# Laying out both segments' triangular blocks over partitions ahead of the substitutions

## Chip, cores and metric

One core of one Trainium2 chip. The metric is the device time of one execution in microseconds (us), as the median of several runs. Engines are named as the profile names them: PE (TensorE), DVE (VectorE), ACT (ScalarE), POOL (GpSimd), SP (SyncE, which only issues transfers here).

## What is computed

A backbone of two layers over two segments of tokens: 512 latent tokens ("lat") and 256 context tokens ("ctx"), width 1024. Each layer normalises its input, multiplies it by one combined input projection, feeds three groups of heads from it (a gated DeltaNet, windowed attention with a sink, an HGRN2 recurrence), projects their joined outputs back, adds them to the stream, and runs a squared-ReLU MLP. The context passes through the same weights and leaves its states for the latents; in the second layer only its states are wanted.

The part that matters here is the triangular system of the DeltaNet scan. For each chunk of 64 tokens, each of 4 heads and each of 2 directions:

```python
a = jnp.where(strict, jnp.einsum('bhid,bhjd->bhij', kb, ki) * decay, 0.0) + eye
uw = lax.linalg.triangular_solve(a, rhs, left_side=True, lower=True, unit_diagonal=True)
```

That is a unit triangular matrix of 64 x 64, to be inverted or solved with. ctx has 4 chunks (32 such matrices), lat has 8 (64 of them).

## The kernel before

**Inverting the blocks.** `delta_prep` builds the strict parts of all matrices on PE, ACT and DVE and leaves them, 64 x 64 each, in one buffer `U` (`seg.U`). `delta_inverse` then inverts them for one segment. It cuts each matrix into four blocks of 32 x 32. The two triangular blocks on the diagonal are laid out one matrix block per partition: 8 n of them, with n = 2 x chunks, so 64 partitions for ctx and 128 for lat. This goes through DRAM, on POOL's queue: one transfer of U to `seg.ud` (L1027) and eight small ones back (L1029), four into buffer P and four into Q. POOL also fills buffer Y with identities (L1024, L1025). DVE copies the half in Q over to P, transposed (L1032), and runs a substitution of 31 steps with two instructions each (L1036, L1037) that turns Y into the inverses; a fourth small buffer, tb, holds the products. DVE makes a transposed copy (L1043), and the results go back through DRAM: two transfers out (L1045), eight back into U (L1048) and four that put the partner blocks of the other orientation into a buffer B (L1050). PE and ACT then finish the off-diagonal blocks in two rounds, one per buffer half: products with B (L1067), a copy to a ring H (L1068), products with H (L1071), and the result into U (L1072). Their PSUM banks are 2 and 3 ("ni").

**What runs beside it.** The line that the change touches, in layer 0, gives the planner three streams: the inverses of ctx and then lat; the rest of the input projections for both segments (`project_hg`, `project_gates`: PE products L554 to L556 with weights that ACT and DVE split at L540 and L541, results written to DRAM by POOL at L748 and L791 from two staging buffers); and attention of ctx (`attention(0, ctx)`: eight rounds, each with scores L1384, a softmax, a transposition L1435, the sums L1444 and a final product on DVE, L1446). After these come two streams for ctx: `delta_chain`, four steps that start with L1103 and L1109 and need the inverted blocks, then `delta_norm`; and `hgrn` with `head_norm`, whose first PE work is L1241, with PSUM banks 2 and 3 again ("hg"), and whose end is L828 to L830. After those come lat's `delta_chain` (eight steps, the same lines), the modulation of the next layer (`ada`, PE at L590, its PSUM bank is 2) and the output projection and MLP of ctx in the background.

**What sets the order.** The streams are Python generators. `run` draws from the stream whose virtual time is least, each `yield` advancing it by an estimate of microseconds divided by a speed. This is the order of tracing, and so the default priority; `ahead(g, 3000)` makes a stream's instructions more urgent. A planner then lays all instructions out against a model of their times and fixes one order for each engine and queue. On the chip each engine takes its instructions in that order and waits where an input or a buffer isn't ready. POOL's transfers and fills are one such queue.

**Buffers.** All work buffers come from one arena in blocks of 1 KB a partition (`get`, `free`). `free` notes a running number. `get` takes the stretch whose newest number is lowest, counted from 30 below the current number, and prefers short free stretches. The bookkeeping follows the order of tracing. An instruction that writes into a reused block waits for those that used it before. P, Q, Y take 4 blocks each and tb one; B takes 2 for ctx and 4 for lat; H takes 2 x 2. ctx attention holds 16 blocks in four rings: two for queries, four for probabilities, three pairs for their transposes, four for the row scales (two of these are used in each round).

Of the kernel before, what the change touches and what calls it, by code (L numbers as in the profile page):

```python
# [167 lines left out]
def bc(ap, axis, n):  # L168
    ap = ap.unsqueeze(axis)
    return ap.broadcast_to(list(ap.shape[:axis]) + [n] + list(ap.shape[axis + 1:]))  # L170
# [103 lines left out]
def run(*streams):  # L274

    at = [[0.0, i, g, speed] for i, (g, speed) in enumerate((x if isinstance(x, tuple) else (x, 1.0)) for x in streams)]
    while at:
        a = min(at)
        try:
            a[0] += next(a[2]) / a[3]  # L280
        except StopIteration:
            at.remove(a)
# [22 lines left out]
class Net:  # L305
# [380 lines left out]
    def project(self, l, segs):  # L686

        for seg in segs:
            if seg.x is None:
                self.x_load(seg)  # L690
        pbs = [self.rstd(seg, "n") for seg in segs]
        if l == 0:
            ring = Ring(self, 8, 1024)
            run(self.ada(0, 0, ring))
            ring.free()
        for seg, pb in zip(segs, pbs):
            seg.h = self.modulated(l, 0, seg, pb)
            self.x_free(seg)
            seg.r, seg.b, seg.need = {}, {}, seg is self.lat or l < DEPTH - 1
            if seg is self.ctx:  # L700
                seg.kv0 = l * 256
# [303 lines left out]
        for x in ("dq", "dk", "dv")[i0:]:  # L1005
            seg.b[x].free()

    def delta_inverse(self, seg):


        nc, Uv = self.nc, seg.U
        n, u = 2 * seg.nc, slice(seg.u0, seg.u0 + 2 * seg.nc)
        half, size = slice(4 * n, 8 * n), slice(0, 8 * n)
        Pb, Qb, Yb, tb = self.get(1024), self.get(1024), self.get(1024), self.get(256)
        P, Q, Y = (b.v.rearrange("p (a b) -> p a b", a=32) for b in (Pb, Qb, Yb))

        def quarters():

            for i in range(8):
                fw, hf, jb = i < 4, i // 2 % 2, i % 2  # L1020
                rows = slice(64 * hf + 32 * jb, 64 * hf + 32 * jb + 32)
                yield slice(i * n, i * n + n), hf if fw else 1 - hf, rows, slice(32 * jb, 32 * jb + 32), fw, fw == (jb == 0)

        nc.gpsimd.memset(Yb.v[size], 0.0)  # L1024
        nc.gpsimd.memset(Yb.v[size, 0:1024:33], 1.0)  # L1025

        nc.gpsimd.dma_start(out=seg.ud[:], in_=Uv[:, :, u])  # L1027
        for blk, vv, rows, cols, fw, first in quarters():
            nc.gpsimd.dma_start(out=(P if fw else Q)[blk], in_=seg.ud[rows, vv, :, cols].rearrange("r u i -> u r i"))  # L1029
        yield 8.0  # L1030

        nc.vector.tensor_copy(P[half], Q[half].rearrange("p a b -> p b a"))  # L1032
        for c in range(31):
            m = 31 - c
            t = tb.v[size, :(c + 1) * m].rearrange("p (r m) -> p r m", m=m)
            nc.vector.tensor_tensor(out=t, in0=bc(Y[size, :c + 1, c], 2, m), in1=bc(P[size, c, c + 1:], 1, c + 1), op=ALU.mult)  # L1036
            nc.vector.tensor_tensor(out=Y[size, :c + 1, c + 1:], in0=Y[size, :c + 1, c + 1:], in1=t, op=ALU.subtract)  # L1037
            yield 0.3 + (c + 1) * m / 480
        Pb.free()
        tb.free()  # L1040
        Z, Bb = Q, self.get(2 * n * 32)
        B = Bb.v.rearrange("p (v u i) -> p v u i", v=2, u=n)
        nc.vector.tensor_copy(Z[size], Y[size].rearrange("p a b -> p b a"))  # L1043
        for i, b in enumerate((Yb, Qb)):
            nc.gpsimd.dma_start(out=seg.xd[i], in_=b.v[size].rearrange("p (a b) -> p a b", a=32))  # L1045

        for blk, vv, rows, cols, fw, first in quarters():
            nc.gpsimd.dma_start(out=Uv[rows, vv, u, cols], in_=seg.xd[0 if fw else 1, blk].rearrange("u r i -> r u i"))  # L1048
            if first:
                nc.gpsimd.dma_start(out=B[rows, vv], in_=seg.xd[1 if fw else 0, blk].rearrange("u r i -> r u i"))  # L1050
        yield 10.0
        Qb.free()
        Yb.free()
        Hr = Ring(self, 2, 512)
        for vv in range(2):
            firsts = []
            for hf in range(2):
                a, b = 64 * hf, 64 * hf + 32
                sa, sb = slice(0, 32), slice(32, 64)
                if hf != vv:  # L1060
                    a, b, sa, sb = b, a, sb, sa
                firsts.append((slice(a, a + 32), slice(b, b + 32), sa, sb))
            ph, pu, H = self.bank("ni"), self.bank("ni"), Hr()
            U = Uv[:, vv, u]
            for ra, rb, sa, sb in firsts:
                for k in range(n):
                    nc.tensor.matmul(ph[rb, k * 32:k * 32 + 32], lhsT=U[ra, k, sb], rhs=B[ra, vv, k], start=True, stop=True)  # L1067
                nc.scalar.copy(H[rb, :n * 32], ph[rb, :n * 32])  # L1068
            for ra, rb, sa, sb in firsts:
                for k in range(n):  # L1070
                    nc.tensor.matmul(pu[ra, k * 32:k * 32 + 32], lhsT=H[rb, k * 32:k * 32 + 32], rhs=U[rb, k, sb], start=True, stop=True)  # L1071
                nc.scalar.activation(out=U[ra, :, sb], in_=pu[ra, :n * 32].rearrange("p (u i) -> p u i", i=32), func=AF.Copy, scale=-1.0)  # L1072
            yield 2.0
        Bb.free()
        Hr.free()
# [436 lines left out]
    def run(self, stop=None):  # L1512
        self.setup()
        lat, ctx = self.lat, self.ctx
        both = (ctx, lat)
# [10 lines left out]
        def seq(*gs):  # L1526
            for g in gs:
                yield from g
# [11 lines left out]
        self.reserve((lat, ctx), "sq0", "sq1")  # L1540
        run(self.ahead(prep(0, both), 3000), (self.project_swa(0, both), 0.6), (ada(0, 2), 0.7))
        self.banks = dict(self.BANKS, m=(4, 5, 6), t=None)
        run(self.ahead(seq(self.delta_inverse(ctx), self.delta_inverse(lat)), 3000), (self.ahead(seq(self.project_hg(0, both), self.project_gates(0, both)), -1000), 0.9), (self.attention(0, ctx), 0.5))
        self.banks = self.BANKS
        for seg in both:
            seg.h.free()
# [115 lines left out]
```

## Time and profile before

| | us |
|---|---|
| median of 3 runs | 2117.33 (2115.97 to 2119.23) |
| the profiled execution | 2116.83 |
| its span in the trace | 2115.0 |
| PE busy | 1977.7 |
| DVE busy | 1219.3 |
| ACT busy | 857.6 |
| POOL busy | 144.2 |

Times in the rows are counted from the start of the span. The profiled execution takes 1.8 us more than its span. A busy PE is not a PE at its peak: its matmuls are pipelined, their ends are modelled, and its clock has two levels, 1.2 and 2.4 GHz. The clock that was granted is given as a share of full speed: 1.00 is 2.4 GHz, 0.50 is 1.2 GHz, values between are a stretch with some of both.

### The profile page before, as it was taken

The numbers are of one execution on the slowest core, as the hardware profiler recorded it, in microseconds if no ns is written. First come the engines' busy times: TensorE is split into PE (matmuls) and PEld (weight loads), VectorE is DVE, ScalarE is ACT, GpSimd is POOL, SyncE is SP. The second block draws the span as 40 slices with busy tenths as digits, with TensorE's granted clock in tenths as the row PEclk, the third lists the DMA queues.
The fourth block names the chain that finished last, engine by engine and source line by source line (L and its number), as shares of the span: only waits on it lengthen the run. The fifth ranks groups of instructions, "written<-read, shape, count | busy, mean of one in ns | idle before, by whom it ended". The sixth has DMA issues, their size and how long they took to land.

```text
span 2115.0 us, 37910 instructions
## 1 busy us (share of the span) xinstructions
PE 1977.7 (94%) x15456; PEld 1620.8 (77%) x15456; DVE 1219.3 (58%) x2737; ACT 857.6 (41%) x1703; POOL 144.2 (7%) x281
## 2 busy tenths in 40 slices
PE   5999998799999999699999998999899979999996
PEld 2787887688899898588888876767678747888885
DVE  4574856666976667577333334666887483333334
ACT  2432353235465564353434242324555234334241
POOL 0001231200000000010000000011200000000000
PEclk9999999799999999899999999999999999999998
DMA  8435342145233243243222235464300222222221
GB/s 336 156 111 165 93 130 77 57 163 188 95 111 106 100 147 111 85 151 105 95 100 94 96 113 187 140 186 154 122 20 2 81 70 91 99 98 92 100 90 70
DMA packets 72445, 242.43 MB, mean 115 GB/s; under 512 B 10192, under 2 KB 12368, under 8 KB 72144
## 3 DMA queue, kind: packets, MB, share of 16 engines
q1 hardware_dynamic: 57456, 197.35, 27.7%
q0 software_dynamic: 11792, 34.14, 5.1%
q10 hardware_dynamic: 3024, 8.53, 1.2%
q8 instruction: 121, 1.98, 0.4%
q14 instruction: 52, 0.43, 0.1%
HBM read 218.21 MB, written 19.14 MB: 112 GB/s over the span
## 4 chain that ended last, share of the span: by engine, by line
PE 78%; DVE 9%; DMA 6%; issue 4%; ACT 2%; POOL 1%; ACTq 0%; DVEq 0%; POOLq 0%
PE psum L554 20%; PE psum L556 19%; PE psum L555 19%; PE psum L590 2%; PE psum L1444 2%; DMA arena<-in_ada 1%; PE psum L1435 1%; PE psum L1382 1%; DVE weights L541 1%; PE psum L1109 1%; PE psum L1067 1%; PE psum L1261 1%; DMA arena<-in_ff 1%; PE psum L1071 1%; DVE arena L1272 1%
## 5 line engine op out<-in xcount | busy, mean ns | idle before, releaser
L554 PE MATMUL psum<-r,weights 128*128 128x512 f32 (+1 forms) x2304 | 830.4, 361 | 11.7 <-ACT arena L725 4.2
L556 PE MATMUL psum<-r,weights 128*128 128x512 f32 (+1 forms) x2304 | 826.6, 360 | 2.1 <-DVE weights L541 2.0
L555 PE MATMUL psum<-r,weights 128*128 128x512 f32 (+1 forms) x2304 | 825.0, 359 | 1.3 <-DVE r L1464 1.0
L540 ACT CAST weights<-arena 128x1024 fp32r<-128x1024 f32 (+3 forms) x295 | 293.3, 995 | 700.1 <-PE psum L555 600.4
L541 DVE TENSOR_TENSOR weights<-arena,weights 128x1024 fp32r<-128x1024 f32 (+3 forms) x295 | 340.5, 1155 | 294.6 <-ACT weights L540 286.4
L554 PEld LDWEIGHTS psum<-r,weights 128*128 128x128 f32 x2304 | 435.9, 189 | 96.1 <-issue 9.6
L556 PEld LDWEIGHTS psum<-r,weights 128*128 128x128 f32 x2304 | 435.8, 189 | 74.2 <-DVE weights L541 6.3
L555 PEld LDWEIGHTS psum<-r,weights 128*128 128x128 f32 x2304 | 435.8, 189 | 70.1 <-issue 3.9
L1492 DVE SCALAR_TENSOR_TENSOR arena<-psum,arena 128x512 f32<-128x512 f32 (+1 forms) x96 | 63.3, 660 | 200.6 <-PE psum L556 200.4
L1488 DVE TENSOR_TENSOR r<-arena,r 128x512 fp32r<-128x512 f32 (+1 forms) x96 | 57.5, 601 | 35.2 <-ACT r L1487 34.8
L653 ACT ACTIVATE r<-arena 128x512 fp32r<-128x512 f32 (+1 forms) x56 | 33.1, 627 | 71.0 <-DVE arena L650 71.0
L590 PE MATMUL psum<-arena 128*32 128x256 f32 x576 | 53.1, 416 | 9.0 <-DMA arena<-in_ada 8.3
L1382 PE MATMUL psum<-r 128*128 128x256 f32 (+1 forms) x256 | 53.6, 320 | 1.7 <-ACT r L1415 1.3
L1486 ACT ACTIVATE arena<-arena 128x512 f32<-128x512 f32 (+1 forms) x96 | 54.0, 564 | 2.4
L1487 ACT CAST r<-arena 128x512 fp32r<-128x512 f32 (+1 forms) x96 | 52.5, 551 | 2.7 <-ACT arena L1428 0.3
L1485 ACT ACTIVATE arena<-psum 128x512 f32<-128x512 f32 (+1 forms) x96 | 50.2, 523 | 0.0
L1472 DVE SCALAR_TENSOR_TENSOR arena<-psum,arena 128x512 f32<-128x512 f32 (+1 forms) x40 | 27.6, 694 | 33.9 <-PE psum L556 33.8
L572 PE MATMUL psum<-weights,r 128*128 128x400 f32 x96 | 35.4, 382 | 10.7 <-DVE arena L650 10.1
L1382 PEld LDWEIGHTS psum<-r 128*128 128x128 f32 x256 | 37.2, 193 | 5.9 <-ACT r L1415 3.2
L590 PE MATMUL psum<-r,arena 128*32 128x256 f32 x192 | 22.8, 491 | 19.0 <-DMA r<-in_ada 19.0
L1402 DVE TENSOR_REDUCE arena<-psum 128x2 f32<-128x512 f32 x40 | 27.5, 687 | 22.2 <-PE psum L1382 18.0
L627 ACT ACTIVATE arena<-arena 128x512 f32<-128x512 f32 (+1 forms) x56 | 30.7, 549 | 22.8 <-DVE arena L1492 11.9
(426 smaller groups left out, 2576.4 us busy)
## 6 DMA issues: line engine op xcount, KB each, us to landing
arena<-in_ff SPq DMA_DIRECT2D x192, 512.0 KB, 3.2
arena<-in_ada SPq DMA_DIRECT2D x72, 512.0 KB, 4.8
arena<-in_win SPq DMA_DIRECT2D x51, 512.0 KB, 4.0
r<-in_ada SPq DMA_DIRECT2D x24, 512.0 KB, 5.2
arena<-in_wout SPq DMA_DIRECT2D x16, 512.0 KB, 3.3
arena<-in_win SPq DMA_DIRECT2D x12, 400.0 KB, 3.6
arena<-in_x ACTq DMA_DIRECT2D x8, 512.0 KB, 7.0
arena<-arena POOLq DMA_DIRECT2D x40, 64.0 KB, 4.6
```

What stands on the lines that cost most here:

```text
L540: nc.scalar.copy(hi, st)
L541: nc.vector.tensor_tensor(out=lo, in0=st, in1=hi.bitcast(F32), op=ALU.subtract)
L554: nc.tensor.matmul(o, lhsT=hi[:, w], rhs=h.hi(k), start=k == 0, stop=False)
L555: nc.tensor.matmul(o, lhsT=hi[:, w], rhs=h.lo(k), start=False, stop=False)
L556: nc.tensor.matmul(o, lhsT=lo[:, w], rhs=h.hi(k), start=False, stop=k == nk - 1)
L590: nc.tensor.matmul(ps[32 * j:32 * j + 32, f * 256:f * 256 + 256], lhsT=self.csil[:, k, :], rhs=st[:, j * 256:j * 256 + 256], start=k == 0, ...
L1382: nc.tensor.matmul(o, lhsT=qs[:, kv], rhs=ks[:, kv, a, c0:c1], start=a == 0, stop=a == 1 and not more)
L1485: nc.scalar.activation(out=t, in_=ps, func=AF.Relu)
L1486: nc.scalar.activation(out=t, in_=t, func=AF.Square)
L1487: nc.scalar.copy(f.hi(k), t)
L1488: nc.vector.tensor_tensor(out=f.lo(k), in0=t, in1=f.hi(k).bitcast(F32), op=ALU.subtract)
L1492: nc.vector.scalar_tensor_tensor(out=seg.x[m], in0=ps, scalar=self.mod(l, 5, m, seg), in1=seg.x[m], op0=ALU.mult, op1=ALU.add)
```

## The change

Layer 0 gives both segments to one call of `delta_inverse`. The old function becomes `delta_blocks`, and a new `delta_inverse` makes one generator of it for each segment, takes the first step of each (everything up to the first `yield`: the buffers P, Q, Y and tb, the fills, the transfers L1027 and L1029), and then runs the generators to their ends, one after the other. So lat's four buffers are taken before those of ctx are freed and before ctx's attention takes its own, and lat's fills and lay-out are traced ahead of ctx's substitution. The two calls in layer 1 have one segment each and trace the same steps as before.

```diff
-    def delta_inverse(self, seg):
-
-
+    def delta_inverse(self, *segs):
+
+
+
+        at = [self.delta_blocks(seg) for seg in segs]
+        for g in at:
+            yield next(g)
+        for g in at:
+            yield from g
+
+    def delta_blocks(self, seg):
         nc, Uv = self.nc, seg.U
         n, u = 2 * seg.nc, slice(seg.u0, seg.u0 + 2 * seg.nc)
         half, size = slice(4 * n, 8 * n), slice(0, 8 * n)
...
-        run(self.ahead(seq(self.delta_inverse(ctx), self.delta_inverse(lat)), 3000), (self.ahead(seq(self.project_hg(0, both), self.project_gates(0, both)), -1000), 0.9), (self.attention(0, ctx), 0.5))
+        run(self.ahead(self.delta_inverse(ctx, lat), 3000), (self.ahead(seq(self.project_hg(0, both), self.project_gates(0, both)), -1000), 0.9), (self.attention(0, ctx), 0.5))
```

## Rows read from the trace of the kernel before

**Rows 1.** Windows by stage: busy us (count) per engine, clock, DMA share, GB/s.
```profile
240.00:273.00 33.00, 33.00 (x214) 28.33 (x213) 29.74 (x90) 11.62 (x31) 8.10 (x14) 1.00 0.39 124
273.00:310.00 37.00, 37.00 (x293) 31.14 (x292) 16.67 (x54) 22.69 (x68) 13.13 (x22) 1.00 0.38 106
310.00:340.00 30.00, 29.79 (x224) 24.99 (x222) 10.08 (x21) 9.73 (x20) 4.72 (x9) 1.00 0.29 101
340.00:371.00 31.00, 21.20 (x452) 19.51 (x452) 28.25 (x86) 10.21 (x26) 3.29 (x7) 0.83 0.21 70
371.00:381.00 10.00, 2.21 (x8) 1.04 (x8) 5.54 (x17) 1.00 (x2) 9.12 (x15) 0.50 0.54 177
381.00:400.00 19.00, 17.60 (x303) 16.81 (x305) 5.23 (x12) 8.17 (x17) 3.81 (x6) 0.54 0.22 61
400.00:446.00 46.00, 43.68 (x960) 39.74 (x957) 36.87 (x119) 13.73 (x34) 1.26 (x2) 1.00 0.08 26
446.00:510.00 64.00, 61.87 (x763) 48.92 (x759) 35.17 (x78) 28.08 (x51) 6.37 (x8) 1.00 0.67 223
```

**Rows 2.** DVE's timeline: start, us, what, idle before and its releaser.
```profile
278.36 1.13 DVE L1032 COPY arena<-arena 64x1024 f32<-64x1024 f32 x1
...
333.09 0.28 DVE L1446 TENSOR_TENSOR r<-psum,arena 128x128 f32<-128x128 f32 x1
...
339.92 0.28 DVE L1446 TENSOR_TENSOR r<-psum,arena 128x128 f32<-128x128 f32 x1
...
341.87 0.18 DVE L1036 TENSOR_TENSOR arena<-arena 128x31 f32<-128x31 f32 x1
...
370.66 0.21 DVE L1037 TENSOR_TENSOR arena<-arena 128x31 f32<-128x31 f32 x1
```

**Rows 3.** POOL's timeline, from 250 to 381 us.
```profile
250.66 0.54 POOL L748 DMA_DIRECT2D hf_ctx<-arena  x1 [1.90 <-ACT arena L745]
...
262.84 0.68 POOL L1027 DMA_DIRECT2D u_lat<-r  x1 [2.34 <-DVE r L998]
267.75 5.01 POOL L1029 DMA_DIRECT2D arena<-u_lat  x8 [4.22 <-PE psum L554]
...
284.39 1.16 POOL L1050 DMA_DIRECT2D arena<-xu_ctx  x2
...
312.96 0.73 POOL L1214 DMA_DIRECT2D arena<-hi_ctx  x1 [15.03 <-PE psum L1067]
...
323.29 0.54 POOL L791 DMA_DIRECT2D dg_lat<-arena  x1 [8.51 <-DVE arena L790]
...
340.26 0.96 POOL L1024 MEMSET arena<- 128x1024 f32 x1
...
375.51 2.63 POOL L1048 DMA_DIRECT2D r<-xu_lat  x4 [0.88 <-DMA xu_lat<-arena]
378.13 2.57 POOL L1050 DMA_DIRECT2D arena<-xu_lat  x4
```

**Rows 4.** Lines between 339 and 446 us: busy us, mean ns, idle before.
```profile
L1109 PE MATMUL psum<-arena,r 128*128 128x128 f32 x72 | 10.9, 298 | 1.7 <-POOL arena L1025 1.7
L1036 DVE TENSOR_TENSOR arena<-arena 128x31 f32<-128x31 f32 (+15 forms) x31 | 10.5, 340 | 0.8
...
L1109 PE MATMUL psum<-r,r 128*128 128x128 f32 x8 | 2.1, 441 | 0.0
```

**Rows 5.** The chain of waits, 381 to 446 us: start, us, what.
```profile
381.73 1.93 PE psum L1067 x32
...
394.19 2.00 PE psum L1109 x8
396.19 1.91 PE psum L1241 x16
398.10 1.23 PE psum L1071 x32
...
445.88 0.40 DVE arena L828
```

## Prediction

> **What bounds the kernel now.** I read the windows by stage first [rows 1]. Up to 340 us PE is full (99.79 of 100 us between 240 and 340) at full clock. From 446 it is full again (61.87 of 64). Between them lies a hole: in 340 to 371 PE is busy 21.20 of 31 us, in 371 to 381 only 2.21 of 10, and in 371 to 400 the clock stands near its lower level, 1.2 GHz (0.50 and 0.54). In the first part of the hole DVE is the full engine (28.25 of 31); before 340 it had room (16.67 of 37 and 10.08 of 30).
>
> DVE's timeline and the groups by line say what fills it [rows 2, 4]: lat's substitution, from 341.87 to 370.87 (370.66 + 0.21), 31 times two instructions of about 340 ns, 21 us in all. Its inputs had long been there. POOL's timeline [rows 3] has lat's U going out at 262.84, the eight lay-out transfers issued from 267.75 to 272.76, and DVE had made its copy by 279.5 [rows 2]. What came late is the fill of Y with identities, at 340.26. I followed the arena's numbers by hand through `get` and `free`: lat's Y takes the blocks of attention's last row-scale buffer, of its two query buffers, and of ctx's tb. The row scale of the eighth round is read last by L1446, 339.92 to 340.20 [rows 2], and the fill follows 0.06 us later. That is the wait.
>
> The chain of waits goes on from there [rows 5]: the results go out and come back on POOL (375.51 to 380.70 for the transfers up to the last with B) [rows 3], PE finishes lat's blocks from 381.73 to about 399.3, and only then are PSUM banks 2 and 3 free for ctx's `hgrn`, which starts at 396.19 and ends with `head_norm` at 446.28. Everything behind it needs its output or bank 2.
>
> **The change part by part.** *The lay-out itself* gains nothing: the same nine transfers, two fills and one copy are issued, and U is not ready before 262.84, so the transfers stay where they are, and POOL's queue is passed by nothing new. No instruction is added.
>
> *The buffers* are the change. All 13 blocks of lat are now taken while ctx's 13 are held and before attention's 16. By the same bookkeeping Y lands on blocks of the decay matrices of `delta_prep`, whose last reader ends when U goes out. So the fill can run near 263 us and the substitution right after the copy, at about 279.5. It needs 62 x 0.34 = 21 us of DVE; the other work takes 26.75 of 67 us there (40%, from the two windows), so it lasts 21 / 0.6 = 35 us and ends by about 315. Is that free for PE? ctx's substitution ran in 240 to 273 with DVE at 29.74 of 33 us, and PE was busy 33.00 of 33 at full clock [rows 1]. I take nothing. The other end: were each of lat's 62 instructions to hold a weight split up by its 0.34 us, 21 us.
>
> POOL issues transfers under this substitution, and its issue of one spill took 0.54 us under ctx's (250.66) and 0.54 with none running (323.29) [rows 3], so I add nothing. The Trainium skill, GPSIMD Engine Reference, section Key points, says that GpSimd shares its SBUF interfaces with VectorE and contends with DVE instructions that have two SBUF inputs, which these are. By that rule POOL would slow down under lat's substitution; the trace shows no such thing for ctx's, and the sum would lose what the fourth rival gives.
>
> *What the buffers push aside.* Nothing else was free, so attention's rings move to the blocks of `dq`, `dk` and `dv` of lat, which are last used when lat's preparation ends, as the rings' old blocks were: nothing. But attention is traced to its end before ctx frees its P, and this puts ctx's B on two row-scale buffers (the seventh round's, read last at 333.09 to 333.37 [rows 2]), ctx's H partly on the last ones (free at 340.20), and lat's B on two of the transposes' (free at about 340). So the tails of both inversions wait for attention's end. For ctx the products move from before 313 to about 340; its chain, which could not start before 340 anyway because the projections held a region of its memory, starts at about 345, and the stretch before 340 loses that much PE work: even.
>
> *The tail of lat.* Its four B transfers can issue at 340.2. In the trace the first products followed their first issue by 381.73 - 378.13 = 3.6 us: now 343.8, say 346 behind ctx's tail. They ran 17.6 us (381.73 to 399.33) at a clock of 0.54; at full clock PE's share scales to 9.5 us, and ACT's copies don't, so I take 14. `hgrn` starts 3 us before the end, as it does now: 346 + 14 - 3 = 357 to 358, against 396.19: **38 us earlier**.
>
> *What is given back.* Lat's chain needs ctx's chain and lat's blocks. It starts at 394.19 now, and six of its eight steps begin before 446: ten groups of 8 at L1109 [rows 4], less four of ctx. Its new start is about 370 (ctx's four steps of some 6 us from 345), so it has 408 - 370 = 38 us beside `hgrn` instead of 52: 4.4 steps. The missing 1.6 fall into the full stretch behind. A step records 120 matmuls, and PE starts one each 48 ns there (960 in 46 us): 5.8 us a step, **9 us**. Three bodies of work now share PE between 345 and 370; I give that 2 us.
>
> The sum: 38 - 9 - 2 = 27 us. Check against PE's hole: idle in 340 to 446 is 9.8 + 7.8 + 1.4 + 2.3 = 21.3 us, the lower clock costs 17%, 50% and 46% of the three busy times, 3.6 + 1.1 + 8.1 = 12.8. No more than about 34 can be won unless PE also packs its small matmuls closer (in 400 to 446 it could take perhaps 8 us more). 27 is four fifths of 34. Behind 446 PE is full, nothing is tied to a fixed time, and the gain travels to the end.
>
> The profiled execution's 2116.83 us less 27 is 2090; it stands 0.5 us under the median of the runs, so this holds for both.
>
> **The rivals.**
>
> *The larger gain, 2075 us.* PE also closes its latency gaps: 34 + 8 = 42 us. For it: the chains are independent from 345 on. Against it: `hgrn` is a chain between PE and DVE, and its 50 us don't shrink.
>
> *A new wait takes most of it, 2105 us.* The tails of both inversions, queued on POOL behind attention's end, come after ctx's chain has begun, and the queue's order, made for modelled times, lets lat's tail end near 384 instead of 360: 12 us remain. For it: B and H of both lie on softmax buffers. Against it: the order near 340 was right in this trace (the fill of Y followed 0.06 us after its release).
>
> *It doesn't do what it says, 2117 us.* Lat's Y again lands on a buffer of attention, the fill stays at 340, and the lay-out was early anyway. Against it: attention takes its rings after lat's Y now.
>
> *POOL slows DVE's neighbour, 2103 us.* If POOL took twice its time under the substitution, its 13.13 us in 273 to 310 [rows 1] would grow by as much, and lat's tail and the spills with it: 27 - 13 = 14 us. [...]
>
> *Slower, 2124 us: ctx's first B transfer blocks POOL.* If the queue keeps it near its place at 284.39 [rows 3], it waits there for the seventh round's end, 333.4: 49 us. Behind it stand the projections' spills, which free two staging buffers, and so PE. A hold of 15.03 us at 312.96 with two spills behind it cost PE nothing (29.79 of 30), so 34 of the 49 would stop PE: 34 - 27 = 7 us slower. It decides once the hold passes 15 + 27 = 42 us. Against it: the planner knows of the wait and will place the transfer near the release it models.
>
> **How the numbers follow.** My forecast, 2081 to 2099, has 52 in 100; the larger gain 14, the new wait 15, POOL's slowing 3, no effect 5, the blocked queue 11. What a measurement of this kernel can tell from no change is 0.2%, about 4 us. Faster: 52 + 14 + 15 + 3 = 84; same 5; slower 11. The likeliest is 2090. The range reaches from the larger gain with a little for buffers that land elsewhere later, 2072, to past the new wait, 2112; it leaves out no effect, slower, and a few in 100 at the edges.
>
> **What would show it.** Right: the fill of Y (128 partitions, L1024) near 263; L1036 and L1037 on 128 partitions between 279 and 318; PE's count of L1241 starting near 357; `head_norm`'s end (L828) near 408; PE's clock at 1.00 through 371 to 400. PE still full before 340. ctx's L1067 close to 340. Wrong: L1024 still at 340 (no effect); L1241 after 375 (new wait); a POOL wait of tens of us at L1050 with PE idle before 340 (blocked queue). What would make it wrong beyond these: buffers later in the kernel that land elsewhere because the numbers in the arena have changed, which can add or remove some us anywhere.

## The result, and the profile after

The changed kernel takes 2103.0 us in the median against 2116.7 us: a ratio of 0.9933 (95% interval 0.9921 to 0.9945), 14 us or 0.67% faster. The profiled execution took 2100.87 us over a span of 2099.0, 16.0 less than before. Below line 1007 the changed file's numbers are 8 higher: L1024 of before is L1032, L1036 and L1037 are L1044 and L1045, L1241 is L1249.

The windows by stage of the changed kernel, with columns as in [rows 1]:

```profile
273.00:310.00 37.00, 37.00 (x244) 31.26 (x243) 31.25 (x104) 20.88 (x63) 12.67 (x22) 1.00 0.37 119
310.00:340.00 30.00, 29.92 (x313) 25.68 (x313) 14.53 (x31) 12.03 (x26) 16.12 (x25) 0.96 0.48 158
340.00:360.00 20.00, 20.00 (x303) 18.94 (x302) 3.24 (x7) 8.51 (x17) 1.14 (x2) 0.50 0.09 29
360.00:381.00 21.00, 19.77 (x473) 17.66 (x469) 16.62 (x40) 6.82 (x17) 1.59 (x3) 0.97 0.20 66
381.00:400.00 19.00, 17.16 (x305) 15.19 (x306) 18.48 (x65) 7.07 (x18) 0.00 (x0) 0.91 0.09 30
400.00:422.00 22.00, 21.97 (x498) 20.61 (x496) 12.90 (x50) 7.25 (x17) 0.53 (x1) 1.00 0.15 51
```

The hole behind 340 is gone: PE has 20.00 of 20 and 19.77 of 21 us where it had 21.20 of 31 and 2.21 of 10 [rows 1]. DVE's work has moved ahead of 340 (31.25 of 37 us instead of 16.67), and PE stayed full there. But 340 to 360 runs at the lower clock, 0.50, though PE is never idle in it.

POOL's timeline, and DVE's first and last step of lat's substitution:

```profile
243.22 0.96 POOL L1032 MEMSET arena<- 128x1024 f32 x1 [5.75 <-PE psum L953]
260.10 0.72 POOL L1035 DMA_DIRECT2D u_lat<-r  x1
265.05 5.00 POOL L1037 DMA_DIRECT2D arena<-u_lat  x8 [4.23 <-PE psum L1392]
293.77 1.19 POOL L1058 DMA_DIRECT2D arena<-xu_ctx  x2 [0.74 <-PE psum L1392]
304.89 1.18 POOL L1058 DMA_DIRECT2D arena<-xu_ctx  x2 [4.92 <-issue]
306.06 0.57 POOL L791 DMA_DIRECT2D dg_lat<-arena  x1
322.56 1.29 POOL L1058 DMA_DIRECT2D arena<-xu_lat  x2 [0.94 <-ACT arena L1436]
334.95 1.33 POOL L1058 DMA_DIRECT2D arena<-xu_lat  x2
```

```profile
278.67 0.18 DVE L1044 TENSOR_TENSOR arena<-arena 128x31 f32<-128x31 f32 x1
313.46 0.21 DVE L1045 TENSOR_TENSOR arena<-arena 128x31 f32<-128x31 f32 x1
```

The fill of lat's Y stands at 243 instead of 340.26 [rows 3], the substitution at 278.7 to 313.7 instead of 341.87 to 370.87 [rows 2]. The B transfers wait for attention's readers (L1392, L1436). The chain of waits, where it passes from lat's tail to ctx's `hgrn`, `head_norm` and the output projection (L590):

```profile
356.74 1.84 PE psum L1079 x32
362.11 1.02 PE psum L1249 x16
419.45 1.14 PE psum L826 x8
422.12 1.00 PE psum L590 x16
```

`hgrn` starts 396.19 - 362.11 = 34.1 us earlier than in [rows 5]. lat's U went out 262.84 - 260.10 = 2.7 us earlier too [rows 3]; that lead is there from the first 50 us on, where the two programs are the same, so it is a difference of the two executions, and 31 us are the change's own. `head_norm`'s last L828 ends at 421.1 instead of 446.3 [rows 5]: 25.2 us, 22.5 net of those 2.7.

```profile
420.18 0.93 DVE L828 SCALAR_TENSOR_TENSOR arena<-arena,psum 128x256 f32<-128x256 f32 x2 [0.81 <-PE psum L826]
```

That gain holds through layer 0 and the start of layer 1. There it shrinks, and two instructions show where: the zero-fills of the two query buffers of lat's `hgrn`, first in the kernel before, then in the changed one:

```profile
1512.74 1.82 POOL L1231 MEMSET r<- 128x2048 f32 x1
1536.20 1.83 POOL L1231 MEMSET arena<- 128x2048 f32 x1
```

```profile
1486.51 1.82 POOL L1239 MEMSET r<- 128x2048 f32 x1
1537.06 1.81 POOL L1239 MEMSET arena<- 128x2048 f32 x1 [27.04 <-issue]
```

The first is 26.2 us earlier, the second 0.9 us later, after POOL had stood still for 27.04 us. The profile names no releaser for that wait; the arena's lists, written out for both kernels, tell what it was. In the kernel before, the second query buffer lies on layer 1's Y and Q, which adjoin there and come free with the inversion's transfers. In the changed kernel Y and Q don't adjoin, and the free stretch of 8 blocks with the oldest numbers is that of the tail's B and H, which PE reads until 1536.94, 0.12 us before the fill. DVE's first scaling of these queries (L1247, now L1255) is then 6.6 us ahead of the kernel before, no longer 26. The changed kernel's last product from H and its scaling, then the scaling of the kernel before:

```profile
1535.75 1.19 PE L1079 MATMUL psum<-arena 32*32 32x32 f32 x32
1539.75 2.47 DVE L1255 TENSOR_TENSOR arena<-r 64x1024 f32<-64x1024 f32 x2
```

```profile
1546.31 2.46 DVE L1247 TENSOR_TENSOR arena<-r 64x1024 f32<-64x1024 f32 x2
```

At the end 16.0 us are left (13.3 net, close to the 14 of the medians).

### The profile page after: what moved, and what is told of

Read it like the earlier page. It is cut to its first block, busy times and chain, and to the rows that moved or that the text cites. A ratio compares the mean times of both kernels' runs of the same rounds, so it can differ in the third digit from the quotient of the medians.

```text
span 2099.0 us, 37907 instructions
## 1 busy us (share of the span) xinstructions
PE 1972.9 (94%) x15456; PEld 1622.8 (77%) x15456; DVE 1216.8 (58%) x2737; ACT 858.1 (41%) x1703; POOL 143.7 (7%) x281
## 4 chain that ended last, share of the span: by engine, by line
PE 80%; DVE 7%; DMA 5%; issue 4%; ACT 2%; POOL 1%; ACTq 0%; DVEq 0%; POOLq 0%; SPq 0%
PE psum L554 20%; PE psum L556 20%; PE psum L555 20%; PE psum L590 2%; PE psum L1452 2%; PE psum L1443 2%; PE psum L1390 1%; DMA arena<-in_ada 1%; PE psum L1117 1%; DVE weights L541 1%; PE psum L1075 1%; PE psum L1079 1%; DMA r<-in_ada 1%; DVE arena L1273 1%; DVE arena L1280 1%
## 5 line engine op out<-in xcount | busy, mean ns | idle before, releaser
L554 PEld LDWEIGHTS psum<-r,weights 128*128 128x128 f32 x2304 | 435.6, 189 | 95.5 <-issue 11.1
L590 PE MATMUL psum<-arena 128*32 128x256 f32 x576 | 51.4, 406 | 9.3 <-DMA arena<-in_ada 8.7
L1494 ACT ACTIVATE arena<-arena 128x512 f32<-128x512 f32 (+1 forms) x96 | 54.1, 564 | 2.4
L572 PE MATMUL psum<-weights,r 128*128 128x400 f32 x96 | 35.0, 378 | 10.7 <-DVE arena L650 10.1
L590 PE MATMUL psum<-r,arena 128*32 128x256 f32 x192 | 23.1, 497 | 19.2 <-DMA r<-in_ada 19.2
L1452 PE MATMUL psum<-arena 128*64 128x128 f32 x456 | 38.7, 294 | 2.2 <-ACT arena L1436 2.2
L650 DVE SCALAR_TENSOR_TENSOR arena<-arena,psum 128x512 f32<-128x512 f32 (+1 forms) x56 | 33.0, 628 | 12.9 <-PE psum L640 12.8
L1448 ACT COPY arena<-psum 128x512 f32<-128x512 f32 x53 | 31.1, 589 | 22.2 <-PE psum L1443 20.8
```

The source lines that it names most:

```text
L554: nc.tensor.matmul(o, lhsT=hi[:, w], rhs=h.hi(k), start=k == 0, stop=False)
L590: nc.tensor.matmul(ps[32 * j:32 * j + 32, f * 256:f * 256 + 256], lhsT=self.csil[:, k, :], rhs=st[:, j * 256:j * 256 + 256], start=k == 0, ...
L1452: nc.tensor.matmul(py[heads[kv]], lhsT=self.vS[:, blocks[k0 + kt], heads[kv]], rhs=PT[:, c:c + 128], start=k0 + kt == 0, stop=k0 + kt == n ...
L1494: nc.scalar.activation(out=t, in_=t, func=AF.Square)
```

## The experiments

Theory P (placing): the gain is where lat's Y lies; what is missing of the forecast is lost in layer 1, by where later buffers lie. Rival T: the gain is the earlier tracing of the lay-out. Rival C (contention): what is missing is lost in layer 0, and later placing is worth nothing.

**Setting all later placing.** The running numbers of the free blocks decide where every later buffer goes. At the end of the inversion stage they are overwritten by those that the other kernel has there (OTHERS stands for that list); the same blocks are free in both.

```diff
+    def ages(self, t):
...
+        self.mem.t, Mem.clock = list(t), 115
...
         self.banks = self.BANKS
+        self.ages(OTHERS)
         for seg in both:
             seg.h.free()
```

*The changed kernel with the numbers of before:*

> The changed kernel, with the ages of the arena's free blocks set, at the end of layer 0's inversion stage, to those that the kernel before has there, so that every later buffer lies where it lay before. Theory P (placing): after the inversion stage the changed kernel stands 26 us ahead, and loses 10 us in layer 1 because the zero-fill of lat's second query buffer in hgrn waits for the inversion tail's buffers; here that fill runs 26 us earlier than in the kernel before, and the time is 2091 (2088 to 2095). Rival C (contention): what is missing of the forecast is lost in layer 0, to the half clock and to VectorE, and later placing is worth nothing: 2101 to 2105.

*The kernel before with the numbers of the changed one:*

> The kernel before, with the ages of the free blocks set, at the end of layer 0's inversion stage, to those of the changed kernel. Theory P: layer 0 stays as it was, and layer 1's zero-fill waits for the tail's buffers as in the changed kernel: 10 us slower than before, 2127 (2121 to 2131). Rival C: no change, 2115 to 2119.

Measured: 2115.8 (ratio 0.9979, 0.9965 to 0.9994) and 2141.2 (1.0098, 1.0078 to 1.0117). Both theories miss the first, and the second is twice P's size. So with the other's placing the changed kernel gives up 10 us of its 14 (0.9979 against 0.9933), and the kernel before 21: each does better with its own. (Runs of different chips are compared here by their ratios to the kernel before; 0.001 is 2.1 us.) The windows show the first loss at once, still in layer 0; the changed kernel, then with the numbers of before:

```profile
380.00:400.00 20.00, 17.81 (x309) 15.41 (x310) 19.48 (x68) 7.97 (x19) 0.00 (x0) 0.91 0.09 28
400.00:420.00 20.00, 19.97 (x451) 18.75 (x450) 11.30 (x46) 6.48 (x16) 0.53 (x1) 1.00 0.13 45
```

```profile
380.00:400.00 20.00, 14.07 (x293) 11.74 (x289) 19.56 (x68) 6.62 (x15) 0.52 (x1) 0.97 0.01 2
400.00:420.00 20.00, 18.03 (x295) 16.30 (x295) 8.34 (x33) 4.26 (x10) 0.54 (x1) 0.78 0.26 81
```

The inversion up to 340 is the same; behind it PE is idle for 5.9 instead of 2.2 us in 380 to 400, and its clock then falls to 0.78. The numbers record which blocks the stage gave back first, and with those of the other kernel the next buffers can land on blocks still in use. That this is what costs the time here is not shown: the waits were not traced further. Rival C falls: later placing is worth much, and 26.2 us of the gain were still there at 1486.5. The consequence for the rest: kernels are compared only where their later placing is the same, or stands as it came out.

**Y alone.** The kernel before, with lat's Y on the four blocks that ctx's Q gives back (15 to 18), traced in the old order:

```diff
-        Pb, Qb, Yb, tb = self.get(1024), self.get(1024), self.get(1024), self.get(256)
+        Pb, Qb, Yb, tb = self.get(1024), self.get(1024), self.get(1024) if y is None else self.at(y, 1024), self.get(256)
```

With later placing as before:

> The kernel before, with one buffer moved: lat's Y lies on the four blocks that ctx's Q gives back, instead of on attention's; lay-out and substitutions are traced in the old order, and later placing is as before. Theory P: the fill runs behind ctx's transfers, at 285 to 297 instead of 340, lat's substitution ends near 330, hgrn starts near 362 as in the changed kernel: 2088 to 2097. Rival T (the trace order ahead of the substitutions is what gains): 2114 to 2118.

With the numbers as they come out:

> As y_only (the kernel before with lat's Y on ctx's Q blocks, and nothing else), but the ages are left as they come out, so that later buffers go where the blocks really came free first. If y_only gained only 3 us because later placing didn't fit the order in which its stage gives blocks back: hgrn at 374 as there, 12 us behind the changed kernel, and in layer 1 the query buffer on Q and Y, which come free early: 2098 to 2106. If a start of hgrn at 374 is worth no more than 3 us whatever the placing: 2113 to 2118.

Measured: 2115.7 (0.9981, 0.9969 to 0.9994) and 2113.7 (0.9966, 0.9952 to 0.9981). The fill moved to 286.56, as P says:

```profile
286.56 0.97 POOL L1034 MEMSET arena<- 128x1024 f32 x1
```

But the substitution ended at 340.1 and not near 330, `hgrn` started at 374.5 and not near 362, and the time expected did not come: 4 us are gained. Yet 2115.7 is what the whole change gives with the same later placing (2115.8): there one moved buffer does as much as the change. `y_nat` gains 7 us, which by its ratio lies between its two expectations; the 3 us by which it is ahead of `y_only` are within the two intervals. The changed kernel, with `hgrn` at 362, has 7 to 10 us more than these two; which part of it is the earlier `hgrn` and which the placing was not separated.

**Everything but Y.** The changed kernel with P and Q of lat laid out ahead as there, but Y taken and filled only when lat's substitution is traced, on the blocks of before; ctx's tail gets H from blocks nobody uses.

```diff
-        Pb, Qb, Yb, tb = self.get(1024), self.get(1024), self.get(1024), self.get(256)
+        Pb, Qb, Yb, tb = self.get(1024), self.get(1024), None if late else self.get(1024), self.get(256)
...
         yield 8.0
+        if late:
+            Yb = self.at(56, 1024)
+            fill(Yb)
```

With later placing as before:

> The changed kernel with P and Q of lat laid out ahead as there, but lat's Y taken and filled only when its substitution is traced, on the blocks that it has in the kernel before (attention's query and row-scale buffers); ctx's tail has buffers that nobody else uses, and later placing is as before. Theory P: the fill waits for attention's end at 340, and the time is that of the kernel before, 2113 to 2119. Rival T: 2089 to 2097.

With later placing as in the changed kernel:

> As y_late (P and Q of lat laid out ahead, its Y late, on attention's buffers), but with later placing as in the changed kernel, so that beside the changed kernel only Y's place and fill, and ctx's tail buffers, differ. Theory P (Y's place is what gains): hgrn of ctx starts near 389 as in y_late, some 27 us later than in the changed kernel, and the time is 16 us or more above the changed kernel's 2103: 2117 to 2128. Rival T (the trace order gains): 2101 to 2106.

Measured: 2131.7 (1.0048, 1.0030 to 1.0066) and 2126.5 (1.0029, 1.0018 to 1.0040). Each has a partner in which only Y's place, its fill and ctx's tail buffers differ: `ages_before` (1.0048 against 0.9979, 15 us) and the changed kernel (1.0029 against 0.9933, 20 us). `y_late_a`'s windows show the hole again:

```profile
340.00:360.00 20.00, 12.32 (x194) 11.23 (x193) 18.10 (x49) 5.63 (x14) 1.08 (x2) 0.77 0.24 81
360.00:380.00 20.00, 3.90 (x73) 3.77 (x74) 4.50 (x14) 0.62 (x2) 12.91 (x19) 0.50 0.39 119
380.00:400.00 20.00, 20.00 (x370) 19.19 (x370) 9.65 (x20) 5.65 (x11) 0.00 (x0) 0.54 0.09 28
```

So T falls: tracing the lay-out ahead without moving Y is no gain, and here 6 to 10 us slower than the kernel before. P had expected the time of the kernel before of `y_late` and misses it by those 10 us; why it is slower was not traced. Beside the rest of the change, Y's place is worth 15 to 20 us, as much as the whole change's 14 or more. (`y_late_a`'s later placing is forced and the changed kernel's is its own, so some of the 20 can be the forcing; in the pair of the 15 both are forced.) Moved by itself in the kernel before, it gained the 4 and 7 us above.

**The tails off attention's buffers.** In layer 0 both tails take B from their own P and H from their own Q; later placing is set to that of the changed kernel:

```diff
-        Z, Bb = Q, self.get(2 * n * 32)
+        Z, Bb = Q, Pb if own else self.get(2 * n * 32)
...
-        Hr = Ring(self, 2, 512)
+        Hr = iter((Qb.v[:, :512], Qb.v[:, 512:])).__next__ if own else Ring(self, 2, 512)
```

> The changed kernel, in which layer 0's tails take their buffers from their own segment: B lies on P, H on Q, instead of on attention's. Later placing is as in the changed kernel. If the tails' wait for attention costs what their 20 us of small matmuls at half clock after 340 show: ctx's tail runs near 297 to 315 and lat's from about 320, beside attention at full clock, hgrn starts near 350 instead of 362, and the time is 2091 to 2096. If PE's work is only moved (it has none to spare before 340): 2100 to 2105.

Measured: 2106.2 (0.9944, 0.9925 to 0.9964), no faster than the changed kernel; the expectation that PE's work is only moved comes nearer.

```profile
340.00:360.00 20.00, 19.96 (x458) 18.77 (x457) 9.82 (x19) 11.77 (x26) 5.12 (x9) 0.91 0.26 74
360.00:380.00 20.00, 18.87 (x438) 16.61 (x434) 18.08 (x49) 7.40 (x18) 1.05 (x2) 1.00 0.16 58
380.00:400.00 20.00, 13.68 (x255) 11.66 (x251) 16.09 (x62) 4.60 (x12) 0.00 (x0) 0.74 0.13 41
```

340 to 360 now runs at 0.91 of the clock, and `hgrn` starts at 355.4, 6.7 us earlier. But `hgrn` and the chain then hold DVE (18.08 of 20 us in 360 to 380), PE stands idle for 6.3 us in 380 to 400 instead of 2.2, and the clock falls to 0.74 there. What the tail's lower clock cost in the changed kernel is lost 30 us later in this one.

**`hgrn` ahead of the chains.** The changed kernel with `self.ahead(seq(self.hgrn(0, ctx, True), self.head_norm(0, ctx)), 2000)` beside the chain:

> The changed kernel with hgrn and head_norm of ctx ahead of the chains in priority. If hgrn takes 59 us instead of 50 there because VectorE is shared with the chain, and that is lost: hgrn ends near 412 instead of 421 and the time is 2093 to 2098. If the chain's steps, which PE must do in any case, only move behind it: 2101 to 2106.

Measured: 2103.3 (0.9916, 0.9903 to 0.9928). `head_norm`'s last L828 ends at 412.7 instead of 421.1, and the time is that of the changed kernel within the two intervals. So `hgrn`'s longer run beside the chain cost nothing that these intervals show: the chain's work, moved behind it, takes as long there.

**Layer 1's query buffer.** Nothing changes until layer 1's inversion, where the same three buffers change roles:

```diff
+        if self.order:
+            b = [self.get(1024) for _ in range(3)]
+            Pb, Qb, Yb = (b[i] for i in (2, 0, 1))
```

The changed kernel, with Q and Y made to adjoin:

> The changed kernel untouched until layer 1's inversion; there Q and Y take the first two of the same three buffers, and P the third, so that they adjoin, and hgrn's second query buffer lies on them as in the kernel before, instead of on the inversion tail's buffers. Theory P1 (the zero-fill that waits for the tail costs the 10 us between 1500 and 1700): 2093, 2090 to 2097, and the zero-fill back at about 1510. Rival S (that stretch would give the time back anyway, to PE or VectorE, which have the same work to do): 2100 to 2105, with the zero-fill early and hgrn's end where it was.

The kernel before, with (1, 0, 2), so that they don't:

> The kernel before, untouched until layer 1's inversion; there P takes the middle one of the three buffers, so that Q and Y don't adjoin and hgrn's second query buffer lies on the tail's buffers, as in the changed kernel. P1: 10 us slower than before, a ratio of 1.003 to 1.007. Rival S: 0.999 to 1.001.

And `own_tail` with (2, 0, 1):

> Both of these: tails on their own segment's buffers in layer 0, and Q and Y adjoining in layer 1. The sum of the two, if each holds: 2080 to 2087.

Measured: 2103.0 (0.9930, 0.9914 to 0.9945), 2126.1 (1.0039, 1.0024 to 1.0054) and 2094.6 (0.9895, 0.9877 to 0.9913). The wait goes where it is sent; the first line is of `l1_apart`, the second of `b_l1_onto`:

```profile
1513.51 1.82 POOL L1244 MEMSET arena<- 128x2048 f32 x1
```

```profile
1563.84 1.80 POOL L1236 MEMSET arena<- 128x2048 f32 x1 [25.86 <-PE psum L1076]
```

It costs the kernel before 8 us, as theory P1 says, and `own_tail` 10 us (0.9944 against 0.9895); `own_l1` misses its sum of 2080 to 2087, because `own_tail` alone had gained nothing. But the changed kernel gets nothing back that can be seen when the wait is taken away, as rival S says: the intervals of 0.9930 and 0.9933 leave room for some 4 us, not for 8. In `l1_apart`'s profile the fill is early and DVE's scaling at 1523.66 instead of 1539.75, and still the first of `hgrn`'s last products start at 1642.2 where they started at 1641.7. Windows of 170 us from the first of the two zero-fills on tell more; the kernel before, the changed one, `l1_apart`, `own_l1`:

```profile
1512.74:1682.74 170.00, 158.92 (x2568) 133.87 (x2569) 121.24 (x339) 86.05 (x243) 15.55 (x22) 0.96 0.16 50
```

```profile
1486.51:1656.51 170.00, 153.08 (x2452) 130.29 (x2453) 118.69 (x333) 84.00 (x238) 15.51 (x22) 0.93 0.15 48
```

```profile
1490.02:1660.02 170.00, 156.22 (x2510) 131.45 (x2512) 119.82 (x335) 84.45 (x240) 15.52 (x22) 0.94 0.16 50
```

```profile
1487.86:1657.86 170.00, 158.63 (x2564) 133.58 (x2565) 121.25 (x338) 84.94 (x242) 15.54 (x22) 0.95 0.16 50
```

PE is idle for 11.1, 16.9, 13.8 and 11.4 us, at a mean clock of 0.96, 0.93, 0.94 and 0.95. In the changed kernel that is 5.8 us of idle time more than before, and, as an estimate, 0.03 x 170 = 5 us for the clock; together about the 10.2 us that it loses from the first fill to the end (26.2 to 16.0). `l1_apart` has 3.1 us less of the idle time but hardly more of the clock, and loses 6.7 us; `own_l1` loses 2.0. Also, `l1_apart` reaches the first fill 3.5 us later than the changed kernel, though up to there the two trace the same steps, so that much is not the wait's. In the profiles of all versions, the six whose second fill waits (26 to 28 us) lose 5.2 to 10.7 us on the kernel before from the first fill to the end, and the seven whose fill doesn't wait lose 2.0 to 6.7. The wait is a cause, then, but part of the 10 us is lost without it too. Why the clock is lower in one version than in another, no run shows.

**The best of them together.** `own_l1` with `hgrn` ahead:

> own_l1 with hgrn and head_norm of ctx ahead of the chains in priority. If that order is worth the 0.2% by which hgrn_first stood beside the changed kernel: a ratio of 0.986 to 0.988 to the kernel before, 2088 to 2092. If it only swaps work that PE must do in any case: that of own_l1, 0.988 to 0.991.

Measured: 2097.3 (0.9901, 0.9883 to 0.9919): the order only swaps work, as in `hgrn_first`. `own_l1`, at 0.9895, has the lowest ratio of all, 8 us under the changed kernel.

## Why the prediction was right, and where it was not

It named the wait, the step that removes it and the direction. 2103 lies in the range of 2072 to 2112, but not in the forecast's own 2081 to 2099, and the gain is 14 us and not 27. That the range holds it is partly luck: its upper end was drawn for a new wait on lat's tail, which did not come.

**The wait**: right. `y_late_a` puts Y back on attention's buffers, and the hole is there again and 20 us are gone.

**"The buffers are the change"**: right, shown by `y_late` and `y_late_a`; from the other side `y_only` equals `ages_before`, but only with later placing as before. The bookkeeping behind it was partly wrong, here and in the section on the change. Attention still takes its rings ahead of lat's blocks, because the other streams are drawn between the two lay-outs, and lat's blocks take the place of `dq`, `dk` and `dv`. The fill so came at 243, not 263. ctx's B went onto the query buffers (released for 293.77 and 304.89) and not the row scales, so ctx's tail was through by 338.6, not after 340, and lat's could begin earlier.

**The substitution**, 279.5 to 315 and free for PE: right (278.7 to 313.7, PE 37.00 of 37).

**POOL's slowing**: didn't happen. POOL was busy 12.67 us in 273 to 310 beside DVE's 31.25, against 13.13 beside 16.67 [rows 1], and a spill's issue took 0.57 us (306.06) against 0.54 [rows 3]. That POOL would take twice its time was an assumption, which no run shows. The rule of the Trainium skill, GPSIMD Engine Reference, Key points, on contention with DVE instructions of two SBUF inputs shows in no issue here.

**The tail**, 38 us: 34.1 measured, 31 net of the early start. Two errors cancel here, which is luck. lat's products began at 336.6, not at 346:

```profile
336.58 1.19 PE L1075 MATMUL psum<-arena,r 32*32 32x32 f32 x29
```

And they took 22 us (to 358.6), not 14. Their clock was taken as full; it was 0.50 from 340 to 360. So they ended near the 360 of the sum, and `hgrn` started 3.5 us behind them, where the sum had it 3 us ahead of their end. In `own_tail` the clock is 0.91 in that stretch, and the time is no better.

**Given back**, 11 us: 34.1 - 25.2 = 8.9 us by the end of `head_norm`. The size is about right, the place is not: the prediction lost it in lat's chain, while it was `hgrn` with `head_norm` that took 59 us instead of 50, with DVE at 18.48 of 19 us in 381 to 400.

**"Behind 446 PE is full, nothing is tied to a fixed time, and the gain travels to the end"**: this step failed. 26.2 us (23.5 net) were still there at 1486.5, close to the forecast, and 10 of them went between there and the end. The prediction named buffers that land elsewhere later as what could make it wrong, and gave it no time. `ages_before` and `b_ages_after` show that later placing as a whole is worth 10 and 21 us, as much as the change. For the 10 us in layer 1, the wait of the zero-fill is shown, and its price in two kernels (8 and 10 us). That it is the price in the changed kernel isn't: without it that kernel is no faster beyond some 4 us. There rival S is right that the stretch gives other losses in its place, but PE's idle time and its clock are counted for one execution only, and the cause of the rest stays open.

Two rivals came near in time for reasons that did not occur. POOL's slowing gave 2103, the time measured, but POOL did not slow; "a new wait" gave 2105, but lat's tail ended at 358.6 and not near 384. The larger gain, no effect and the blocked queue are out.

## What to carry to other kernels

Where an allocator reuses buffers by age, a change to the order of tracing is two changes: the waits at the place itself, and a new layout of everything after it. Write out both allocators' lists to the end, look for large buffers that now lie on something read late, and give that a price, for it can be as large as the change. To test one cause, hold the later layout equal in both kernels; but a layout fits the order in which its own stage gives blocks back, so a forced one can have a cost of its own.

## What was not expected

PE busy without a gap ran at the lower clock: 20.00 of 20 us at 0.50 in 340 to 360, two thirds of them (202 of 303 recorded) products of 32 x 32:

```profile
L1079 PE MATMUL psum<-r,arena 32*32 32x32 f32 x128 | 7.6, 237 | 0.0
L1075 PE MATMUL psum<-arena,r 32*32 32x32 f32 x74 | 4.5, 237 | 0.0
```

In `own_tail` the same stretch holds as many of them (211 of 458), with more products of the chain among them, and ran at 0.91. So a full PE in the busy column is not a PE at full clock; the clock's column has to be read with it.
